# A decoder layer on one core: attention's queries and keys by tokens, one set of angle tables, and retention's gates by turns with the mixer gates

## The chip, the cores and the metric

The kernel runs on one core of one Trainium2 chip. The metric is the device time of one execution in microseconds (us); the figure given is the median of several executions. One further execution of the same program is recorded by the hardware profiler, and all views of the trace come from that one.

## What is computed

One layer for 256 tokens of 2048 features, all in float32: a half feed-forward, a pair of gated token mixers side by side (retention with 8 heads, sliding-window attention with 16 query heads and 4 key heads), a second half feed-forward, and a gated embedding. The part that the change touches, cut from the reference:

```python
rq, rk, rv, rg, aq, ak, av, gate_r, gate_a = jnp.split(h @ w_in[i], SPLIT_POINTS, axis=-1)
# columns: 1024, 1024, 2048, 2048, 1024, 256, 256, 2048, 2048

rq = rotary(rq.reshape(B, S, RET_HEADS, RET_DK), positions, RET_DK, RET_THETA)
rk = rotary(rk.reshape(B, S, RET_HEADS, RET_DK), positions, RET_DK, RET_THETA) * (RET_DK ** -0.5)
ro = head_group_norm(retention_chunkwise(rq, rk, rv), ret_gn_g[i])
ret_branch = (jax.nn.silu(rg) * ro) @ w_ret_out[i]

aq = rotary(aq.reshape(B, S, ATT_HEADS, ATT_DH), positions, ROPE_DIMS, ROPE_THETA)  # 16 of 64
ak = rotary(ak.reshape(B, S, ATT_KV_HEADS, ATT_DH), positions, ROPE_DIMS, ROPE_THETA)
att_branch = sliding_window_attention_sinks(aq, ak, av, att_sinks[i]) @ w_att_out[i]

mixed = (jax.nn.sigmoid(gate_r) * ret_branch + jax.nn.sigmoid(gate_a) * att_branch) @ w_mix_out[i]
```

`rotary` turns pairs of features by an angle that depends on the token's position: all 128 features of a retention head (64 angles), and the first 16 of an attention head (8 angles).

## The kernel before

**Weights.** The weights stream in from memory as tiles of 128 x 1024 floats. For float32 accuracy each is cut in two: ACT casts a high part (L162, tiles named hw), DVE subtracts it from the raw tile for the low part (L164, lw), and PE adds three matmuls for each product (L510 to L512). Where two neighbouring pairs of columns and rows allow it, a unit called Seven makes sums of raw tiles on DVE (L279 to L298; tiles uw, vw, bw and their halves huw, luw, hvw, lvw) and needs seven products in place of eight.

**The planner.** Units of work are planned ahead in a list. `fill` issues a unit's load on SP's queue and, later, its casts, as long as there is room: `slots_for_weights(n)` sets how many tiles may be held (24 for the first stage of the mixers, 14 from rq to the aqk stage, 18 in gt, 22 behind). Casts are issued when less than 45 units of time stand ready, an ordinary tile being 12. After each unit `run_side` takes one step from the list `side` and advances the generators `slow` and `lazy` by one step each. So what a list holds, and in which order the code calls the projections, sets the order on every engine.

**Order of the mixers.** rv01 (two of four blocks of retention's values), rq, rk, rv23, four blocks of retention's gates rg with retention's own steps in `side`, av, five groups aqk (attention's keys, then the queries) with attention's steps in `side`, four blocks gt (columns of the mixer gates), then the gates ga0 and ga1 as blocks with Seven units.

**By tokens and by features.** Most projections are computed by tokens: the tile of tokens is the stationary operand and 512 weight columns stream past. rq and rk are such blocks (`mixer_block`) of 4 x 256 columns with two Seven units each; their result is rotated by tokens (L1393 to L1401) and then turned by a DMA transpose between two passes of ACT (`Turn`, L227, L231, L238), since the scores need features on partitions. aq and ak are computed by features instead (`features_out`, L455 to L490): the weights are stationary and the tokens stream, so that the result has features on partitions at once. A chunk is 8 matmuls over 512 columns, which hold the high and low parts of the 256 tokens (L461), and 8 over 256 columns (L469). `joined` (L1287) adds the two halves, and `turn_by_angle` (L1293 to L1297) rotates with a shuffle of partitions.

**Angle tables.** `rotary_table` (L986) is run once for retention and once for attention: it computes angles for 256 tokens by features, [128 x 256]. Retention's are then transposed on PE (L1378) to have them by tokens.

**Steps.** Retention's head passes through ret1 (scores, L1479), ret1b (decay and split into rsp, L1483), ret2 (outputs ro, L1504) and normalisation; attention through att1 (scores, L1611), att1b (mask and maxima), att1c (Exp, L1633 and L1638), att2 (its transposes, L227 and L231), att2b (outputs ao, L1680) and att3. Silu of rg is at L1576.

Of the kernel before, what the change touches and what calls it, by code (L numbers as in the profile page):

```python
# [70 lines left out]
def layer(ctx: ExitStack, tc: tile.TileContext, io):  # L71
# [281 lines left out]
    def sums_ahead(items, wait, every):  # L353
# [9 lines left out]
        for j, (key, _) in enumerate(items):  # L363
            a, b = pairs.pop()
            b11, b21, b12, b22 = a.of(a.raw, 0), a.of(a.raw, 1), b.of(b.raw, 0), b.of(b.raw, 1)
            u, v = (slot([P, 2, 512], F32, w + a.name) for w in "uv")
            t1, t3, t2, t4 = (x.rearrange("p (g n) -> p g n", g=2) for x in (u[:, 0], u[:, 1], v[:, 0], v[:, 1]))
            parts = [slot([P, 2, 512], F32R, w + a.name) for w in ("hu", "lu", "hv", "lv")]
            uh, ul, vh, vl = parts
            away = [dram.tile([P, 2, 512], F32, name=f"{w}{a.name}") for w in ("hud", "lud", "hvd", "lvd")]  # L370
            put_by_sums[key] = away
            dve.tensor_tensor(t1, b11, b12, ALU.add)
            dve.tensor_tensor(t3, b12, b22, ALU.add)
            yield from pause()
            act.copy(uh, u)
            dve.tensor_tensor(t2, b11, t3, ALU.add)
            dve.tensor_tensor(t4, t2, b21, ALU.add)
            yield from pause()
            act.copy(vh, v)
            if j + 1 < len(items):  # L380
                pairs.append([Chunk(k) for k in items[j + 1]])
            dve.tensor_tensor(ul, u, uh, ALU.subtract)
            yield from pause()
            dve.tensor_tensor(vl, v, vh, ALU.subtract)
            for e in range(2):
                sync.dma_start(away[e], parts[e].bitcast(F32))
            yield from pause()
            for e in range(2, 4):
                sync.dma_start(away[e], parts[e].bitcast(F32))
# [62 lines left out]

    def features_chunk(key, n_k, rhs, ps):
        c, chunks = key[-1], n_k // 4
        u = take(key)  # L455
        hi, lo = u.chunk.hi, u.chunk.lo

        def high(kk):
            k = 4 * c + kk
            for f in range(2):  # L460
                pe.matmul(  # L461
                    ps[f], hi[:, kk, f * P : (f + 1) * P], rhs(k),
                    start=k == 0, stop=k == n_k - 1,
                )

        def low(kk):
            k = 4 * c + kk
            for f in range(2):
                pe.matmul(  # L469
                    ps[f][:, :S], lo[:, kk, f * P : (f + 1) * P], rhs(k)[:, :S],  # L470
                    start=False, stop=False,
                )

        for kk in range(3):
            high(kk)
        if c < chunks - 1:
            high(3)
            for kk in range(4):
                low(kk)
        else:  # L480
            for kk in range(4):
                low(kk)
            high(3)
        done(u)
        run_side()

    def features_out(groups, n_k, rhs, before=None):

        for c in range(n_k // 4):
            if before is not None:
                before(c)
            for key, ps in groups:
                features_chunk(key + (c,), n_k, rhs, ps)
# [146 lines left out]

    def plan_features(keys, n_k):
        for c in range(n_k // 4):
            for key in keys:
                plan.append(Single(key + (c,)))
# [322 lines left out]
    trig = {}  # L969
# [16 lines left out]
    def rotary_table(nm):  # L986

        inv, sgn = (0, 2) if nm == "r" else (1, 3)
        pos_i = slot([P, S], I32, "pos_i" + nm)
        act.dma_start(pos_i, io["positions"].broadcast_to([P, S]))  # L990
        pos = slot([P, S], F32, "pos" + nm)
        yield
        dve.tensor_copy(pos, pos_i)
        table = slot([P, 2, S], F32, "trig" + nm)
        cos, sin = trig[nm] = table[:, 0, :], table[:, 1, :]
        w = slot([P, 4, S], F32, "rot" + nm)
        ang, n, na, nb = (w[:, j, :] for j in range(4))
        dve.tensor_scalar(ang, pos, cst[:, inv : inv + 1], None, ALU.mult)
# [6 lines left out]
        for who, j in ((na, 0), (nb, 0), (na, 1), (nb, 1), (na, 2), (nb, 2), (na, 3)):  # L1005
            dve.scalar_tensor_tensor(ang, who, -TWO_PI[j], ang, ALU.mult, ALU.add)
            if who is nb:
                yield
        yield
        dve.tensor_scalar(n, ang, 3.1415925, -3.1415925, ALU.min, ALU.max)  # L1010
        yield
        act.activation(nb, n, AF.Sin)
        yield
        dve.tensor_scalar(sin, nb, cst[:, sgn : sgn + 1], None, ALU.mult)
        dve.tensor_scalar(na, ang, 1.5707963267948966, None, ALU.add)
        dve.tensor_scalar(n, na, 3.141592653589793, -6.283185307179586, ALU.is_gt, ALU.mult)
        dve.tensor_tensor(na, na, n, ALU.add)
        dve.tensor_scalar(na, na, 3.1415925, -3.1415925, ALU.min, ALU.max)
        yield
        act.activation(cos, na, AF.Sin)  # L1020
# [262 lines left out]
    def joined(ps, name, dst=None):  # L1283
        lo = half(name + "lo")
        v = half(name + "v") if dst is None else dst
        for f in range(2):
            act.copy(lo[:, f], ps[f][:, S:])  # L1287
            dve.tensor_tensor(v[:, f], ps[f][:, :S], lo[:, f], ALU.add)
        return v

    def turn_by_angle(q, name, dst, cos, sin, shuffle):
        qs = half(name + "sh")
        dve.stream_shuffle(qs, q, shuffle)  # L1293
        c, s = (v[:, None, :].broadcast_to([P, 2, S]) for v in (cos, sin))
        dve.tensor_tensor(q, q, c, ALU.mult)
        dve.tensor_tensor(qs, qs, s, ALU.mult)
        dve.tensor_tensor(dst, q, qs, ALU.add)  # L1297

    def rotate(ps, name, dst, cos, sin, shuffle):
        turn_by_angle(joined(ps, name), name, dst, cos, sin, shuffle)  # L1300

    SH_R = [(i + 16) % 32 for i in range(32)]
    SH_A = [i + 8 if i < 8 else i - 8 if i < 16 else i for i in range(32)]
# [3 lines left out]
    QK_UNITS = [units_of(order, SEVEN[: order.count("S")]) for order in ("PPPSPSPP", "PPSPSPPP")]  # L1307
    qk_keys = lambda b: lambda n, p: ("w_in_f2", 4 * b + 2 * n, p)
# [5 lines left out]
    def plan_mixers():  # L1314
        block_units([("P", p) for p in range(KD // 2)], lambda n, p: ("w_rv", n, p))
        for b in range(2):
            block_units(QK_UNITS[b], qk_keys(b))
        for blk in range(2, 4):
            plan_tokens(("w_rv", blk), KD)
        for grp in range(8, 16, 2):  # L1320
            plan_tokens(("w_in_f2", grp), KD)
        plan_tokens(("w_av",), KD, nk=4)
        for grp in (20, 16, 17, 18, 19):
            plan_features([("w_in_f", grp)], KD)
        for grp in range(21, 29, 2):
            plan_tokens(("w_in_f2", grp), KD)
# [16 lines left out]
    def mixers(ht, norm, residual, keepers, away):  # L1343
        rhs = lambda k: (ht[:, k, :S], ht[:, k, S:])
        both_halves = lambda k: ht[:, k, :]
        rq, rk = [], []
        made = {}
        forms = lambda p: made[p // 2](p % 2)
        sums_of, wide = {}, {}
# [23 lines left out]
        def wide_tables():  # L1373
            cos, sin = trig["r"]
            ps = bank("rtab").rearrange("p (w t n) -> p w t n", w=2, t=2)
            for j, v in enumerate((cos, sin)):
                for t in range(2):
                    pe.transpose(ps[:, j, t], v[:, t * P : t * P + P], ident)  # L1378
            for j, w in enumerate("cs"):
                wide[w] = slot([P, 2, 512], F32, f"rtab{w}")  # L1380
                for t in range(2):
                    act.copy(
                        wide[w][:, t].rearrange("p (h n) -> p h n", h=4), ps[:, j, t][:, None, :].broadcast_to([P, 4, P])
                    )

        def rotated(v, name, to):
            halves = lambda x: x.rearrange("p t (q two n) -> p two (t q) n", two=2, n=16)
            crossed = {}

            def cross():  # L1390
                x = crossed["x"] = slot([P, 2, 512], F32, name + "x")
                for two in range(2):
                    dve.tensor_tensor(  # L1393
                        halves(x)[:, two], halves(v)[:, 1 - two], halves(wide["s"])[:, two], ALU.mult
                    )

            def scale():
                dve.tensor_tensor(v, v, wide["c"], ALU.mult)

            def add():  # L1400
                dve.tensor_tensor(v, v, crossed.pop("x"), ALU.add)  # L1401
                crossed["t"] = Turn(v, name)

            def join():
                to.append(slot([P, 4, S], F32, name + "t"))
                crossed.pop("t").join(to[-1])

            return [
                cross, scale, add, lambda: crossed["t"].part(), lambda: crossed["t"].move(), idle, join,
            ]  # L1410
# [708 lines left out]
```

## Time and profile before

| | |
|---|---|
| median of 3 runs | 2221.23 us (2220.66 to 2221.66) |
| profiled execution | 2221.96 us, of which the span of the trace is 2220.0 us |
| mixers' first stage (rv01) to the end of gt | 692.5 to 1138.2 us |
| rq, rk | 737.80 to 780.46, 780.46 to 822.62 us |
| rv23 | 822.62 to 866.14 us |
| rg with retention | 866.14 to 968.28 us |
| av, aqk with attention, gt with attention | to 979.80, 1039.56, 1138.17 us |

A row of a view begins with the engine or the place in time; L12 is a line of the kernel; names such as hw_in_f are the program's tiles, with an arrow from what an instruction reads to what it writes. PE's rows of matmuls overlap, so that the distance between starts (0.23 us for 512 columns) and not the length shown (0.39) is what one costs. SPq is the queue that SP issues DMAs from.

### The profile page before, as it was taken

To read this page: it belongs to the slowest core of one execution; us is meant where nothing else is said; L and a number is where in the kernel's file an instruction comes from. 1 tells how busy PE (TensorE), PEld (TensorE's weight loads), DVE (VectorE), ACT (ScalarE), POOL (GpSimd) and SP (SyncE) were. 2 spreads that over 40 slices of the span, in tenths; PEclk is the share of its full clock that TensorE was granted. 3 is DMA by queue.
4 is the path that set the end of the run, shared out by engine and by line. 5 is a ranking of instruction groups with operands and counts; after the bars stand their busy time and mean duration, and the time that the engine had idled before them with its cause. 6 is when DMAs were issued, how large, how long until landed. Compare 5 with 4: busy or idle time off the path is not lost.

```text
span 2220.0 us, 28845 instructions
## 1 busy us (share of the span) xinstructions
PE 2209.2 (100%) x9980; PEld 1825.5 (82%) x9980; DVE 2021.5 (91%) x2620; ACT 1475.5 (66%) x1706; POOL 48.4 (2%) x62
## 2 busy tenths in 40 slices
PE   9999999999999999999999999999999999999998
PEld 7888888888888888888788888888888878888887
DVE  6999999999988997998999888779999999899887
ACT  5877777777565656666866566466767678765653
POOL 0000000000000000000000000000000000000000
PEclk9999999999999999999999999999999999999999
DMA  9989889977686779886977478788899988767771
GB/s 316 271 224 266 248 246 258 252 241 237 222 301 231 260 266 324 271 296 219 302 223 242 166 226 328 298 299 276 289 314 312 289 264 268 215 236 240 282 291 70
DMA packets 315754, 576.00 MB, mean 259 GB/s; under 512 B 107084, under 2 KB 112076, under 8 KB 315608
## 3 DMA queue, kind: packets, MB, share of 16 engines
q1 hardware_dynamic: 305992, 543.79, 73.0%
q0 software_dynamic: 7632, 27.79, 6.7%
q10 hardware_dynamic: 1984, 2.58, 0.3%
q8 instruction: 78, 1.28, 0.2%
q14 instruction: 68, 0.56, 0.1%
HBM read 490.20 MB, written 33.55 MB: 236 GB/s over the span
## 4 chain that ended last, share of the span: by engine, by line
PE 94%; DMA 3%; DVE 2%; ACT 1%; issue 1%; SPq 0%; ACTq 0%; DVEq 0%
PE f1g L510 3%; PE f1g L512 3%; PE f1g L511 3%; PE f2g L510 2%; PE f1u L511 2%; PE f1u L510 2%; PE f1u L512 2%; PE f2g L511 2%; PE f2g L512 2%; PE f2u L512 2%; PE f2u L510 2%; PE f2u L511 2%; PE aqk L461 2%; PE f1e L512 1%; PE f2d L510 1%; PE f1d L512 1%
## 5 line engine op out<-in xcount | busy, mean ns | idle before, releaser
L164 DVE TENSOR_TENSOR lf_gu<-rf_gu,hf_gu 128x1024 fp32r<-128x1024 f32 x123 | 145.3, 1219 | 17.9 <-ACT hf_gu L162 17.2
L164 DVE TENSOR_TENSOR lw_in_f<-rw_in_f,hw_in_f 128x1024 fp32r<-128x1024 f32 x124 | 148.5, 1218 | 11.2 <-ACT hw_in_f L162 11.2
L162 ACT CAST hf_gu<-rf_gu 128x1024 fp32r<-128x1024 f32 x123 | 123.6, 1048 | 24.8 <-DMA rf_gu<-in_f_gu 24.8
L284 ACT CAST huf_gu<-uf_gu 128x1024 fp32r<-128x1024 f32 x83 | 87.3, 1052 | 76.7 <-DVE uf_gu L280 65.5
L293 ACT CAST hvf_gu<-vf_gu 128x1024 fp32r<-128x1024 f32 x83 | 87.5, 1054 | 76.0 <-DVE vf_gu L289 65.7
L164 DVE TENSOR_TENSOR lf_down<-rf_down,hf_down 128x1024 fp32r<-128x1024 f32 x96 | 115.8, 1220 | 22.3 <-ACT hf_down L162 18.8
L162 ACT CAST hw_in_f<-rw_in_f 128x1024 fp32r<-128x1024 f32 x124 | 125.8, 1048 | 11.3 <-DMA rw_in_f<-in_w_in_f 7.7
L162 ACT CAST hf_down<-rf_down 128x1024 fp32r<-128x1024 f32 x96 | 98.4, 1049 | 29.5 <-DMA rf_down<-in_f_down 13.4
L298 DVE TENSOR_TENSOR lvf_gu<-vf_gu,hvf_gu 128x1024 fp32r<-128x1024 f32 x83 | 101.0, 1217 | 0.0
L296 DVE TENSOR_TENSOR luf_gu<-uf_gu,huf_gu 128x1024 fp32r<-128x1024 f32 x83 | 101.0, 1217 | 0.0
L287 DVE TENSOR_TENSOR lf_gu<-rf_gu,hf_gu 128x1024 fp32r<-128x1024 f32 x83 | 101.0, 1217 | 0.0
L277 ACT CAST hf_gu<-rf_gu 128x1024 fp32r<-128x1024 f32 x83 | 86.8, 1046 | 5.9 <-DMA rf_gu<-in_f_gu 3.2
L510 PE MATMUL f1g<-hf_gu,xt 128*128 128x512 f32 x223 | 87.0, 390 | 1.4 <-ACT hf_gu L113 1.4
L512 PE MATMUL f1g<-lf_gu,xt 128*128 128x512 f32 x223 | 86.9, 390 | 0.0
L511 PE MATMUL f1g<-hf_gu,xt 128*128 128x512 f32 x223 | 86.8, 389 | 0.0
L510 PE MATMUL f2g<-hf_gu,ht 128*128 128x512 f32 x196 | 76.4, 390 | 0.0
L512 PE MATMUL f2g<-lf_gu,ht 128*128 128x512 f32 x196 | 76.3, 389 | 0.0
L511 PE MATMUL f2g<-hf_gu,ht 128*128 128x512 f32 x196 | 76.3, 389 | 0.0
L510 PE MATMUL f1u<-hf_gu,xt 128*128 128x512 f32 x180 | 70.0, 389 | 0.0
L511 PE MATMUL f1u<-hf_gu,xt 128*128 128x512 f32 x180 | 70.0, 389 | 0.0
L512 PE MATMUL f1u<-lf_gu,xt 128*128 128x512 f32 x180 | 70.0, 389 | 0.0
L182 POOL DMA_DIRECT2D lf_gu<-rf_gu x37 | 32.2, 871 | 1630.4 <-ACT lf_gu L181 1365.3
(1640 smaller groups left out, 7310.0 us busy)
## 6 DMA issues: line engine op xcount, KB each, us to landing
rf_gu<-in_f_gu SPq DMA_DIRECT2D x362, 512.0 KB
rf_down<-in_f_down SPq DMA_DIRECT2D x176, 512.0 KB
rw_in_f<-in_w_in_f SPq DMA_DIRECT2D x148, 512.0 KB
lf_gu<-rf_gu POOLq DMA_DIRECT2D x37, 512.0 KB, 8.6
rw_rv<-in_w_rv SPq DMA_DIRECT2D x32, 512.0 KB
rw_ret<-in_w_ret SPq DMA_DIRECT2D x32, 512.0 KB
rw_mix<-in_w_mix SPq DMA_DIRECT2D x32, 512.0 KB
rw_pg<-in_w_pg SPq DMA_DIRECT2D x32, 512.0 KB
```

Of the source, the lines that this page charges most:

```text
L162: act.copy(c.hi, c.raw)
L164: dve.tensor_tensor(c.lo, c.raw, c.hi, ALU.subtract)
L277: act.copy(a.hi, a.raw)
L284: act.copy(uh, u)
L287: dve.tensor_tensor(a.lo, a.raw, a.hi, ALU.subtract)
L293: act.copy(vh, v)
L296: dve.tensor_tensor(ul, u, uh, ALU.subtract)
L298: dve.tensor_tensor(vl, v, vh, ALU.subtract)
L461: pe.matmul(ps[f], hi[:, kk, f * P : (f + 1) * P], rhs(k), start=k == 0, stop=k == n_k - 1,)
L510: pe.matmul(o, al, bh, start=first, stop=False)
L511: pe.matmul(o, ah, bh, start=False, stop=False)
L512: pe.matmul(o, ah, bl, start=False, stop=self.left == 0)
```

## The change

1. aq (1024 columns) becomes a third block by tokens behind rk, with two Seven units; ak (256 columns) follows it, also by tokens, as 96 matmuls of 256 columns. Both are rotated by tokens and then turned by DMA transposes (three more of these). The functions for projections by features are gone.
2. One generator, `rotary_tables`, computes all 72 angles by tokens, [128 x 144], at the start; it spreads the inverse frequencies over tokens by two PE transposes. The second pass for attention, which ran beside rg, is gone.
3. The order is rv01, rq, rk, aq, ak, rv23, av, and then rg0, gt0, rg1, gt1, rg2, gt2, rg3, gt3. All steps of retention and attention lie in one list of 72 places, of which one is taken after each unit from av on. Room for weights is 16 tiles in ak and rv23, and 12 from av to gt3.
4. The side work `sums_ahead` (sums of the second feed-forward's weights, stored to memory and read later) makes three in rq, rk and aq, three in ak, rv23 and av, and four within rg and gt; its tiles are taken one at a time. All of gt's results are copied by ACT, where DVE did two of four. The decay tables load one at a time.

```diff
+    QK_UNITS = [units_of(order, SEVEN[: order.count("S")]) for order in ("PPPSPSPP", "PPSPSPPP", "PPSPSPPP")]
+    qk_keys = lambda b: lambda n, p: ("w_in_f2", (0, 4, 16)[b] + 2 * n, p)
...
+        for b in range(3):
+            name = ("rq", "rk", "aq")[b]
+            got = mixer_block(name, QK_UNITS[b], qk_keys(b), rhs)
...
+            side.extend(both_rotated(got, name, (rq, rk, aq)[b], name[0]))
+        slots_for_weights(16)
+        akv = slot([P, 4, S], F32, "akv")
+        ps = banks("ak")
+        tokens_out(("w_in_f", 20), KD, rhs, ps, n=256)
...
+        side.extend(rotated(ak, "ak", lambda: akv[:, 0:2, :], "a"))
...
-        for grp in (20, 16):
-            attention_features(grp)
...
+        more = sums_ahead(ahead[6:10], 0, 1)
+        at = [[] for _ in range(72)]
+        for m in range(8):
+            for j, part in zip((0, 2, 4, 5, 6, 8, 11), (att1, att1b, att1c, att2, att2a, att2b, att3)):
+                at[1 + 8 * m + j].append(part(m))
+        for c in range(4):
+            h = 2 * c
+            for j, part in (
+                (0, ret1(h)), (2, ret1b(h)), (2, ret1(h + 1)), (4, ret1b(h + 1)), (4, ret2(h)), (7, ret2(h + 1)),
+                (8, ret2b(c)), (12, ret2c(c)), (14, ret3(c)), (15, ret3a(c)), (19, ret3b(c)),
+            ):
+                at[4 + 16 * c + j].append(part)
...
+        slots_for_weights(12)
+        slow.append(spread_out())
...
+        for j in range(4):
+            ps = banks(f"rg{j}")
+            paired_out(("w_in_f2", 8 + 2 * j), KD, rhs, ps)
...
+                act.activation(g[:, t], ps[t], AF.Silu)
...
+            ps = banks(f"gt{j}")
+            paired_out(("w_in_f2", 21 + 2 * j), KD, rhs, ps)
+            sig.append(slot([P, 2, 512], F32, f"sig{j}"))
...
+                act.copy(sig[-1][:, t], ps[t])
```

PE, at the attention queries. Before, the first chunk by features behind av (numbers at the ends of names count buffers):

```order
L512 MATMUL av_8715<-lw_av_8667,ht_5993 128x256
L461 MATMUL aqk_8849<-ht_5993,hw_in_f_0_8740 128x512
L461 MATMUL aqk_8850<-ht_5993,hw_in_f_0_8740 128x512
L461 MATMUL aqk_8849<-ht_5993,hw_in_f_0_8740 128x512
...
L469 MATMUL aqk_8849<-ht_5993,lw_in_f_0_8741 128x256
L469 MATMUL aqk_8850<-ht_5993,lw_in_f_0_8741 128x256
L469 MATMUL aqk_8849<-ht_5993,lw_in_f_0_8741 128x256
```

Now, the first of the queries' rows, directly behind rk's last (aqa and aqb are the two halves of tokens):

```order
L472 MATMUL rka_6907<-lw_in_f_6_7_7191,ht_5993 128x512
L470 MATMUL rkb_6909<-hw_in_f_6_7_7190,ht_5993 128x512
L471 MATMUL rkb_6909<-hw_in_f_6_7_7190,ht_5993 128x512
L472 MATMUL rkb_6909<-lw_in_f_6_7_7191,ht_5993 128x512
L470 MATMUL aqa_7296<-hw_in_f_16_2_7211,ht_5993 128x512
L471 MATMUL aqa_7296<-hw_in_f_16_2_7211,ht_5993 128x512
L472 MATMUL aqa_7296<-lw_in_f_16_2_7212,ht_5993 128x512
L470 MATMUL aqb_7298<-hw_in_f_16_2_7211,ht_5993 128x512
L471 MATMUL aqb_7298<-hw_in_f_16_2_7211,ht_5993 128x512
L472 MATMUL aqb_7298<-lw_in_f_16_2_7212,ht_5993 128x512
```

The queries have moved from behind av to behind rk, weights and tokens have changed places, and each is now three wide matmuls.

ACT, beside the attention's Exp of one head group. Before, within aqk (the load of the table with Exp stands here and nowhere else in this part of the program; aes and asc are the sink's and the scores' tiles):

```order
L162 CAST hw_in_f_0_9202<-rw_in_f_0_9088 128x1024
L1633 ACT_TABLE_LOAD
L1633 ACTIVATE aes_9149<-aes_9149 128x4
L1638 ACTIVATE asc_9140,asm_9209<-asc_9140,anm_9147 128x128 x2
L1638 ACTIVATE asc_9140,asm_9209<-asc_9140,anm_9147 128x256 x2
L162 CAST hw_in_f_1_9230<-rw_in_f_1_9110 128x1024
L162 CAST hw_in_f_2_9258<-rw_in_f_2_9132 128x1024
L227 COPY wat_9264<-asc_9140 128x768 x2
```

Now, between rg1 and gt1 (23_3 is the gates' weight tile, rgs the Silu of retention's gate):

```order
L162 CAST hw_in_f_23_3_9090<-rw_in_f_23_3_9029 128x1024
L1556 ACTIVATE aes_9049<-aes_9049 128x4
L1561 ACTIVATE asc_9040,asm_9097<-asc_9040,anm_9047 128x128 x2
L1561 ACTIVATE asc_9040,asm_9097<-asc_9040,anm_9047 128x256 x2
L1654 ACT_TABLE_LOAD
L1654 ACTIVATE rgs_9117<-rg_8853 128x512
L1654 ACTIVATE rgs_9117<-rg_8854 128x512
L162 CAST hw_in_f_23_4_9134<-rw_in_f_23_4_9067 128x1024
```

Exp and Silu now stand next to each other, and a table load goes ahead of each change from one to the other.

SP, where gt ends and the first Seven unit of the gates (tiles 29_0 and 31_0) is loaded. Before:

```order
L127 DMA rw_in_f_29_4_10261<-in_w_in_f 128x2x512
L386 DMA hudf_gu_0_4_10085<-huf_gu_0_4_10081 128x1024
L386 DMA ludf_gu_0_4_10086<-luf_gu_0_4_10082 128x1024
L127 DMA rw_in_f_31_4_10288<-in_w_in_f 128x2x512
L127 DMA rw_in_f_29_5_10319<-in_w_in_f 128x2x512
L389 DMA hvdf_gu_0_4_10087<-hvf_gu_0_4_10083 128x1024
L389 DMA lvdf_gu_0_4_10088<-lvf_gu_0_4_10084 128x1024
L127 DMA rw_in_f_31_5_10342<-in_w_in_f 128x2x512
L231 DMA_TRANSPOSE mat_10344<-wat_10321 128x12x128
L127 DMA rw_in_f_29_0_10362<-in_w_in_f 128x2x512
L127 DMA rw_in_f_31_0_10364<-in_w_in_f 128x2x512
```

Now (mro is retention's transposed output; hudf to lvdf are sums stored for later):

```order
L127 DMA rw_in_f_29_4_10238<-in_w_in_f 128x2x512
L127 DMA rw_in_f_31_4_10271<-in_w_in_f 128x2x512
L231 DMA_TRANSPOSE mat_10273<-wat_10240 128x12x128
L127 DMA rw_in_f_29_5_10299<-in_w_in_f 128x2x512
L127 DMA rw_in_f_31_5_10318<-in_w_in_f 128x2x512
L231 DMA_TRANSPOSE mro_10358<-wro_10339 128x16x128
L388 DMA hudf_gu_0_4_10095<-huf_gu_0_4_10243 128x1024
L388 DMA ludf_gu_0_4_10096<-luf_gu_0_4_10276 128x1024
L393 DMA hvdf_gu_0_4_10097<-hvf_gu_0_4_10275 128x1024
L393 DMA lvdf_gu_0_4_10098<-lvf_gu_0_4_10360 128x1024
L127 DMA rw_in_f_29_0_10385<-in_w_in_f 128x2x512
L127 DMA rw_in_f_31_0_10387<-in_w_in_f 128x2x512
```

The loads of 29_0 and 31_0 now stand behind both transposes and the four stores, which are not spread among the earlier loads any more.

More of the change, by code (lines that the diff above doesn't have):

```diff
@@ L451, in run_side @@
                 jobs.pop(0)
[L453 to L495, printed above, removed]
     class Sum:
@@ L1700, in mixers @@
[L1700 to L1704 removed]
+            for j, part in zip((0, 2, 4, 5, 6, 8, 11), (att1, att1b, att1c, att2, att2a, att2b, att3)):
[7 more added lines that the diff above has]
+                at[4 + 16 * c + j].append(part)
+            for j in (6, 10, 11, 15):
+                at[4 + 16 * c + j].append(lambda: next(more, None))
+            if c < 3:
+                at[4 + 16 * c + 9].append(lambda c=c: load_decay(c + 1))
@@ new lines, in mixers, with spread_out @@
+        at[67].append(lambda: next(more, None))
+        for step in range(2):
+            at[4 + 3 * 16 + 10 + step].append(lambda step=step: forms_step(1, step))
+        def spread_out():
+            for jobs in at:
+                for f in jobs:
+                    f()
+                yield
+        slots_for_weights(12)
+        slow.append(spread_out())
+        ps = banks("av")
+        tokens_out(("w_av",), KD, rhs, ps, n=256)
+        for t in range(2):
+            dve.tensor_copy(akv[:, 2 + t, :], ps[t][:, :S])
```

285 lines of the change are left out of this document (117 added, 168 removed).

## The prediction

> **What bounds the kernel now.** I read the page's head first, then its chain of work that ended last, then TensorE's waits, and then a table of busy time by stage.
>
> ```profile
> span 2220.0 us, 28845 instructions
> PE 2209.2 (100%) x9980; PEld 1825.5 (82%) x9980; DVE 2021.5 (91%) x2620; ACT 1475.5 (66%) x1706; POOL 48.4 (2%) x62
> PE 94%; DMA 3%; DVE 2%; ACT 1%; issue 1%; SPq 0%; ACTq 0%; DVEq 0%
> ```
>
> PE is busy for 2209.2 of 2220.0 us and holds 94% of the chain. So the time is PE's own work plus about 11 us, and an edit counts only by PE work that it removes, or by a wait on PE that it makes. All weights reach PE through ACT (the rounded high part) and DVE (the rest), and DVE stands at 91%: it is the engine that can become late. In the stages that the change rearranges, PE waits for one thing alone (the rows of waits: what waited for what, us in total, times, longest):
>
> ```profile
> PE ro L1504 <- DVE rsp L114: 0.5, 1, 0.5
> DVE lw_in_f L164 <- ACT hw_in_f L162: 9.7, 13, 2.3
> ```
>
> The first row is the only PE wait from 690 to 1180 us; the second is DVE's own wait from 866.1 to 1138.2 us, needed below. The stages, as a table (stretch, length, then busy us and instructions of PE, weight loads, DVE, ACT, POOL, granted clock, DMA share, GB/s):
>
> ```profile
> 780.50:822.60 42.10, 42.10 (x187) 34.88 (x186) 41.83 (x48) 28.14 (x29) 0.00 (x0) 1.00 0.73 230
> 866.10:968.30 102.20, 101.67 (x490) 85.37 (x490) 95.57 (x186) 65.03 (x81) 0.00 (x0) 1.00 0.86 289
> 968.30:979.80 11.50, 11.50 (x98) 11.50 (x97) 10.83 (x24) 7.18 (x11) 0.00 (x0) 1.00 0.59 236
> 979.80:1039.60 59.80, 59.80 (x355) 51.25 (x353) 50.14 (x84) 38.23 (x63) 0.00 (x0) 1.00 0.73 243
> 1039.60:1138.20 98.60, 98.60 (x483) 77.71 (x481) 90.86 (x163) 79.46 (x139) 0.00 (x0) 1.00 0.95 292
> ```
>
> They are: retention's keys (rk); rg with retention; av; the old queries and keys by features (aqk); the mixer gates (gt) with attention. PE is full in each. The clock was granted in full (1.00). In rk DVE is full as well, 41.83 of 42.10.
>
> **PE work: queries and keys by tokens.** The old form, from the chain (start, us, what):
>
> ```profile
> 979.96 1.84 PE aqk L461 x8
> 981.80 0.95 PE aqk L469 x8
> 982.75 1.84 PE aqk L461 x8
> ```
>
> A chunk is 8 wide and 8 narrow matmuls, 1.84 + 0.95 = 2.79 us. There are 5 groups of 4 chunks: 20 x 2.79 = 55.8 us. The new queries are a third block with two units of seven products in place of eight, as rk is: 186 matmuls, so the length of rk's row, 42.1. The new keys are 96 narrow matmuls, as av is: 11.5. That is 53.6, so **-2.2 us**. It is the only large term that is sure; it rests on counts and on rows of the same shapes.
>
> **Small PE terms.** The angle tables lose two of four transposes:
>
> ```profile
> 746.13 0.44 PE rtab L1378 x4
> ```
>
> so -0.2. Attention's and retention's small matmuls break into the stream of weights. Where that happens:
>
> ```profile
> 1137.04 0.39 PE L512 MATMUL gt<-lw_in_f,ht 128*128 128x512 f32 x1
> 1137.36 0.66 PE L1680 MATMUL ao<-apt,akv 128*64 128x256 f32 x4
> 1138.17 0.50 PE L510 MATMUL ga0a<-hw_in_f,ht 128*128 128x512 f32 x1
> ```
>
> From 1137.04 to 1137.36 is 0.32 us against 0.23 from one wide matmul to the next, so a changeover costs some 0.1. The scores of one head group and the outputs of another no longer stand together, which makes three more interruptions: **+0.3**. Retention's own waits may go:
>
> ```profile
> 934.55 0.56 DVE rsp L114
> 935.15 1.34 PE ro L1504 x9
> 939.24 1.07 PE ro L1504 x9
> ```
>
> One group took 1.34 for 1.07 behind DVE's rsp, and with the 0.5 of the wait row that is about 0.8 in the stage. With two more steps between scores and outputs I take **-0.8**; if DVE is as late as before it is 0, and the same wait at all eight groups would be +4. PE work and its old waits sum to -2.2 - 0.2 + 0.3 - 0.8 = **-2.9**.
>
> **What DVE must now do in a row: rq, rk, aq.** So far the values' projection, light on DVE, followed rk. Now a third block of the same kind does. How far DVE is ahead shows in the end of a low part and PE's first use of it, in three pairs:
>
> ```profile
> 772.54 1.22 DVE L164 TENSOR_TENSOR lw_in_f<-rw_in_f,hw_in_f 128x1024 fp32r<-128x1024 f32 x1
> 780.91 0.39 PE L512 MATMUL rka<-lw_in_f,ht 128*128 128x512 f32 x1
> 800.61 1.22 DVE L298 TENSOR_TENSOR lvw_in_f<-vw_in_f,hvw_in_f 128x1024 fp32r<-128x1024 f32 x1
> 803.35 0.39 PE L512 MATMUL rks<-lvw_in_f,gaf0h 128*128 128x512 f32 x1
> 817.01 1.22 DVE L164 TENSOR_TENSOR lw_rv<-rw_rv,hw_rv 128x1024 fp32r<-128x1024 f32 x1
> 823.07 0.39 PE L512 MATMUL rv<-lw_rv,ht 128*128 128x512 f32 x1
> ```
>
> The lead is 780.91 - 773.76 = 7.15 us at rk's start, 803.35 - 801.83 = 1.52 behind its second unit of seven, and 823.07 - 818.23 = 4.84 at its end. rk thus spends 5.6 of lead in its middle. If aq starts with 4.84 and spends the same (rk's rotation falls in it, as rq's falls in rk), PE stands for 5.6 - 4.84 = 0.8. The lower bound is 0, since the sums made on the side are spread otherwise. The upper is 4: aq begins with nothing ahead but what the first plain units win back (about 2). I take **+0.7**, near the pairs.
>
> **av, then rg and gt by turns, with every step of both mixers beside them.** The room for weights falls from 14 and 18 to 12. Loads run 6 units ahead, not 8, a unit of 12 matmuls being 12 x 0.227 = 2.7 us; the casts keep their distance of 4 units. What DVE drops with the old form:
>
> ```profile
> L164 DVE TENSOR_TENSOR lw_in_f<-rw_in_f,hw_in_f 128x1024 fp32r<-128x1024 f32 x22 | 26.1, 1219 | 3.0 <-ACT hw_in_f L162 3.0
> L1288 DVE TENSOR_TENSOR ra0v<-aqk,ra0lo 128x256 f32<-128x256 f32 x2 | 0.8, 420 | 1.8 <-ACT ra0lo L1287 1.8
> L1293 DVE STREAM_SHUFFLE ra0sh<-ra0v 128x512 f32<-128x512 f32 x1 | 0.8, 751 | 0.0
> L1296 DVE TENSOR_TENSOR ra0sh<-ra0sh,triga 128x512 f32<-128x512 f32 x1 | 0.7, 683 | 0.0
> ```
>
> Over the four old stages DVE was busy 95.57 + 10.83 + 50.14 + 90.86 = 247.4 us. Off go 26.1 of low parts and five rotations of 0.8 + 0.8 + 3 x 0.7 = 3.7, 18.5 in all. 203 remain for a stretch of 102.2 + 11.5 + 98.6 = 212.3: 96%. That hides in PE's time with 9 us left. If the cover goes, each us over is one of PE's. ACT: 189.9 before, less 20 casts and the copies (about 24), plus what follows.
>
> ```profile
> 1014.90 1.06 ACT L162 CAST hw_in_f<-rw_in_f 128x1024 fp32r<-128x1024 f32 x1
> 1015.98 1.28 ACT L1633 ACT_TABLE_LOAD   x1
> 1017.27 0.21 ACT L1633 ACTIVATE aes<-aes 128x4 f32<-128x4 f32 x1
> ```
>
> Silu and Exp now alternate on ACT, 8 table loads instead of 1: 7 x 1.28 = 9.0 us. ACT then stands at about 176 of 212 us (83%), so I cost them at nothing; the cover is the lead of the casts, 4 units or 11 us, against two loads that stand at most a few us apart. The cast before the load ended at 1015.96 and the next instruction began at 1017.27, so the row holds the whole price here.
>
> The Trainium skill, page "ScalarE: Activation LUTs", section "Table sets: the hidden batching unit", speaks against this change: "Batch activation calls by **set**, not by function". Its section "What ACT_TABLE_LOAD costs" puts a drain of some 1.38 us on top of the load; the trace shows the load's 1.28 us and no drain. By the page the seven switches would be an estimated 18.6 us of ACT, which would still fit.
>
> For the whole stretch I take **+0.2**: 0 below, 5 above.
>
> **Gates' first unit of seven.** In the new order its two raw tiles wait for a place that the last gt unit frees, and stand behind two transposes and four stores on SP's queue. Before:
>
> ```profile
> 1128.21 1.71 SPq L231 DMA_TRANSPOSE mat<-wat  x1
> 1130.01 17.57 SPq L127 DMA_DIRECT2D rw_in_f<-in_w_in_f  x8
> 1139.05 1.05 ACT L277 CAST hw_in_f<-rw_in_f 128x1024 fp32r<-128x1024 f32 x1
> 1142.69 1.22 DVE L287 TENSOR_TENSOR lw_in_f<-rw_in_f,hw_in_f 128x1024 fp32r<-128x1024 f32 x1
> 1149.68 0.39 PE L512 MATMUL ga0s<-lw_in_f,ht 128*128 128x512 f32 x1
> ```
>
> Issue was at 1130.01, the cast at 1139.05, the low part ready at 1143.91, used at 1149.68: 19.7 us from issue to use, 5.8 of them spare. Now the issue comes about when gt ends (1138.17, above), 11.5 before the use: 8.2 later against 5.8 spare, 2.4 late if the chain keeps its length. But the cast stood behind one that waited for PE, not for its data, so the chain can be shorter. Bounds 0 and 4; I take **+1.0**. The three more DMA transposes (1.71 on SP each) stand in stretches where loads are 6 units ahead: 0.
>
> **Sum.** -2.9 + 0.7 + 0.2 + 1.0 = -1.0 us. From the profiled execution's 2221.96 (span 2220.0 and 2.0 around it) that is 2221.0; the median of the runs, 2221.23, lies 0.7 below that execution, so the forecast is **2220.2**.
>
> **Rivals.**
> 1. *All stalls hidden.* The three waits of 0.7, 0.2 and 1.0 don't come: -2.9, so 2218.3. For it: one PE wait in 490 us so far. Against: leads of 1.5 us. Chance 0.22.
> 2. *The gates' unit or aq's block late in full*, +4 at one of them: -1.0 + 3 is 2223.2. Chance 0.14.
> 3. *Slower: DVE the bound in rg and gt.* It needs 203 of 212.3 us; its waits for ACT's casts were 9.7 in these stages. With table loads and all steps ahead of casts those waits could double, to 203 + 19 = 222, 10 over, of which the lead at the start (some 4) is spent first: +6, so 2226.2. It decides where DVE's waits pass 13 us, the 9 free and the lead of 4. For it: DVE at 95.57 of 102.20 already. Against: steps are spread evenly, which shortens waits. Chance 0.14.
> 4. *Slower: ACT switching.* The casts come late by the loads themselves; all seven on PE's path would be +9.0, 2229. Against: ACT keeps 36 us free. Chance 0.04. That is the case that the Trainium skill's rule on sets would make.
> 5. *The saving isn't there*, because the third block or the new keys take as long as the old form: +2.2, 2222.4. Counts and equal shapes speak against. Chance 0.04.
>
> **How the numbers follow.** The forecast has 0.42, the rivals 0.22, 0.14, 0.14, 0.04 and 0.04. About 0.2% (4.4 us) is what a measurement of this kernel can tell from no change. Faster by more needs under 2216.8, beyond even the first rival: 0.06. Slower by more needs over 2225.7: most of rival 3, rival 4 and a little of rival 2, 0.18. The rest, 0.76, is within. The range runs from 2217.0 (rival 1 with another 1.3 of interruptions saved) to 2226.8 (rival 3 with its place).
>
> **What would show it.** Right: aq's block takes 42 to 43 us and ak 11.5; the row of PE waiting for rsp is gone; the table loads stand beside a PE without waits; PE's waits in ga0 are under 2 us. Wrong: waits of PE for lw_in_f in aq (third term), for lw_in_f or hw_in_f within rg and gt (rivals 3 and 4, told apart by whether DVE waits for ACT there), or a wait at the first ga0s matmul above 3 (rival 2). What would make the whole wrong is a stall spread in pieces too small for rows of waits: then PE's stages are longer than their counts at 0.227 a matmul.

## The result

The changed kernel takes 2252.0 us (median of 4 runs, 2250.3 to 2253.5) against 2221.3 us before: 1.0138 times as long, interval 1.0121 to 1.0156. It is 31 us slower, where 1 us faster was forecast, and lies outside the range. The profiled execution took 2251.16 us. The head of its page and its chain:

```profile
span 2249.1 us, 28774 instructions
PE 2218.7 (99%) x9940; PEld 1826.0 (81%) x9940; DVE 2008.3 (89%) x2593; ACT 1496.3 (67%) x1730; POOL 48.3 (2%) x62
PE 77%; DVE 4%; DMA 4%; ACT 2%; issue 1%; SPq 0%; ACTq 0%; DVEq 0%
```

PE has fallen from 94% of the chain to 77%, though DVE has less to do than before and ACT, with 20.8 us more, is busy for only 67% of the span: the sum of the work is not what made it slower. PE is shown busy for 9.5 us more with fewer matmuls, so some of them ran longer. The largest of its waits from 865 to 1210 us, where before had one of 0.5:

```profile
PE as L1534 <- ACT akv L238: 4.9, 1, 4.9
PE ga0s L470 <- ACT hw_in_f L277: 4.4, 1, 4.4
PE ga0s L472 <- DVE lw_in_f L287: 3.9, 3, 2.2
PE ro L1469 <- DVE rsp L114: 3.2, 3, 2.0
PE ga0s L472 <- DVE luw_in_f L296: 1.4, 1, 1.4
PE rv L472 <- DVE lw_rv L164: 1.1, 1, 1.1
```

And rows of the table by stage: ga0 before, then, in the changed kernel, aq, av, the third rg block and ga0:

```profile
1138.20:1179.10 40.90, 40.90 (x182) 33.85 (x181) 40.26 (x50) 25.21 (x29) 0.00 (x0) 1.00 0.64 211
821.20:865.10 43.90, 42.70 (x187) 34.73 (x186) 42.64 (x51) 28.63 (x30) 0.00 (x0) 1.00 0.91 282
921.50:941.30 19.80, 14.86 (x106) 13.93 (x106) 15.93 (x24) 16.15 (x26) 0.00 (x0) 0.83 1.03 340
1043.50:1073.10 29.60, 27.61 (x139) 22.12 (x138) 21.17 (x42) 23.98 (x38) 0.00 (x0) 1.00 0.94 297
1148.50:1209.30 60.80, 49.98 (x189) 36.74 (x189) 48.21 (x58) 35.26 (x43) 0.00 (x0) 0.89 0.66 225
```

av has 11.5 us of weight matmuls and lasts 19.8; ga0 took 41.0 before and takes 60.8. In both the granted clock is below 1, 0.83 and 0.89. From the first matmul of rv01 to the last of ga0, by the starts of PE's rows:

| part | before | after | difference |
|---|---|---|---|
| rv01, rq, rk | 130.1 | 129.9 | -0.2 |
| aqk's own matmuls, now aq and ak | 56.4 | 55.5 | -0.9 |
| rv23 | 43.5 | 44.9 | +1.4 |
| av's own matmuls | 11.5 | 18.1 | +6.6 |
| rg, gt and all small matmuls up to gt's end | 204.2 | 208.9 | +4.7 |
| ga0 | 41.0 | 60.8 | +19.8 |
| sum | 486.7 | 518.1 | +31.4 |

The rest of the program, which the change does not touch, is 2.2 us shorter in this execution, so the two profiled executions differ by 29.2. Two stages hold 26 of the 31 us.

**ga0.** What SP did around gt's end, at 1148.5 us (start, us, queue, line, DMA):

```profile
1141.37 1.44 SPq L231 DMA_TRANSPOSE mat<-wat  x1
1142.91 1.39 SPq L127 DMA_DIRECT2D rw_in_f<-in_w_in_f  x2
1152.68 1.76 SPq L231 DMA_TRANSPOSE mro<-wro  x1
...
1157.19 1.11 SPq L393 DMA_DIRECT2D lvdf_gu<-lvf_gu  x1
1158.39 6.59 SPq L127 DMA_DIRECT2D rw_in_f<-in_w_in_f  x8
```

The queue issues in order. Nothing leaves it from 1144.3 to 1152.68, because the transpose of retention's last output waits for ACT's copy of it, which ends at 1152.65. From there the queue issues without a pause: the transpose and the four stores take it until 1158.3 (the low part that the last store reads is ready at 1156.0, before the queue comes to it). Only then, 9.9 us after gt's end, come the eight loads for the gates: 4.1 us of this are the wait, the rest is the issue of the five DMAs. ACT can cast the first tile 6 us later:

```profile
1164.63 1.04 ACT L277 CAST hw_in_f<-rw_in_f 128x1024 fp32r<-128x1024 f32 x1 [9.93 <-DMA rw_in_f<-in_w_in_f]
```

ACT had stood for 9.93 us with nothing to cast, DVE for 10.05, and PE waits seven times in the rest of the stage. Of the 19.8 us, 10.8 are waits of PE and 0.8 are attention's last outputs, which now fall in ga0; the other 8.2 us are its products themselves, which run longer, in part at half the granted clock (last section).

**av.** The chain of waits at the end of rv23 and in av:

```profile
908.13 11.03 DMA rf_gu<-in_f_gu
...
921.85 0.15 DVE ak L1363
922.26 0.35 issue
922.62 0.61 ACT wak L227
923.26 7.77 DMA mak<-wak
931.08 0.61 issue
931.68 0.75 ACT akv L238
932.48 0.80 PE as L1534 x4
```

rf_gu is a raw tile of the second feed-forward, for a sum that is only stored for later. DVE, in order, stood for 5.7 us at that sum with the keys' rotation behind it. The keys were then turned late, and the first scores of attention, which stand in PE's order ahead of the rest of av, held PE for 4.9 us. The window from 865 to 945 us has three such waits on DVE:

```profile
DVE uf_gu L372 <- DMA rf_gu<-in_f_gu: 14.8, 3, 7.7
```

So two queues that work in order, SP's and DVE's, each held something urgent behind something that was not. That is the theory to test; its rival is that DVE or ACT has too much to do in the new order. Against the rival stands already that from av to gt's end, 227.0 us, DVE is busy for 179.7 and ACT for 165.5.

### The profile page after: what moved, and what is told of

It reads as the page before. It is cut to its first block, busy times and chain, and to the rows that moved or that the text cites. A ratio compares the mean times of both kernels' runs of the same rounds, so it can differ in the third digit from the quotient of the medians.

```text
span 2249.1 us, 28774 instructions
## 1 busy us (share of the span) xinstructions
PE 2218.7 (99%) x9940; PEld 1826.0 (81%) x9940; DVE 2008.3 (89%) x2593; ACT 1496.3 (67%) x1730; POOL 48.3 (2%) x62
## 3 DMA queue, kind: packets, MB, share of 16 engines
q8 instruction: 78, 1.28, 0.2%
## 4 chain that ended last, share of the span: by engine, by line
PE 77%; DVE 4%; DMA 4%; ACT 2%; issue 1%; SPq 0%; ACTq 0%; DVEq 0%
PE f2g L472 2%; PE f2g L471 2%; PE f2g L470 2%; PE f2u L472 2%; PE f2u L470 2%; PE f2u L471 2%; DMA rw_in_f<-in_w_in_f 1%; PE f2e L472 1%; PE f2e L470 1%; PE f1e L472 1%; PE f2d L470 1%; PE f1e L470 1%; PE f1d L470 1%; PE f2d L471 1%; PE f1d L471 1%; PE f1d L472 1%
## 5 line engine op out<-in xcount | busy, mean ns | idle before, releaser
L279 DVE TENSOR_TENSOR uf_gu<-rf_gu 128x512 f32<-128x512 f32 x83 | 56.8, 684 | 12.6 <-DMA rf_gu<-in_f_gu 9.3
```

## Experiments

All are made from the changed kernel unless said; before was timed beside each (medians 2221.5 us for experiments 1 to 4, 2222.2 for 5 to 8, 2221.7 for 9 to 11). Stages are read from one profiled execution of each kernel.

**1. Room for the gates' loads.**

```diff
             ps = banks(f"gt{j}")
+            if j == 3:
+                slots_for_weights(16)
```

> The changed kernel with room for 16 weight tiles in place of 12 from the last gt block on. Theory A (the loads of the gates' first unit of seven stand too late in SP's queue, behind a transpose and four stores, because there is no room for them sooner): they now stand ahead of those, PE's waits in ga0 fall from about 10.8 us to under 2, ga0 takes 41 to 44 us in place of 60.8, and the time falls by 16 to 19 us, to 2233 to 2236. Rival (ACT or DVE cannot keep up with rg and gt by turns, and ga0 only pays what they left undone): casts and low parts are late whatever is loaded, ga0 stays above 50 us, the time above 2242.

Measured: 2243.2 us, ratio to before 1.0097 (1.0082 to 1.0112). The first loads of the unit of seven were issued at 1145.3, ahead of the transpose of retention's output, and the wait of 4.4 us is gone. But only half of the expected gain came:

```profile
1152.50:1201.60 49.10, 46.12 (x189) 35.70 (x188) 46.56 (x57) 33.54 (x41) 0.00 (x0) 0.93 0.74 249
```

DVE is at 46.56 of 49.10 here: with the queue mended, the retention and attention steps that had slipped into ga0 fill it. The rival has a share in this stage: the time is where it had put it, ga0 just under its 50 us.

**2. The queue's order alone.** Room stays 12; retention's last transpose and the last stored sums go five places later.

```diff
-                at[4 + 16 * c + j].append(part)
+                at[4 + 16 * c + j + (5 if c == 3 and j > 13 else 0)].append(part)
...
-                at[4 + 16 * c + j].append(lambda: next(more, None))
+                at[4 + 16 * c + j + (5 if c == 3 and j > 10 else 0)].append(lambda: next(more, None))
...
-        at[67].append(lambda: next(more, None))
+        at[73].append(lambda: next(more, None))
```

> The changed kernel, room still 12, with retention's last transposes five places later and the last stored sums five places later, so that both stand behind the loads of the gates' first unit of seven in SP's queue. Theory A in its narrow form (the queue's order, not the room): the loads issue when gt ends instead of 10 us later, ga0 takes 43 to 50 us, the time is 2235 to 2242. Rival (room for 12 tiles alone makes the unit late): ga0 stays within 3 us of 60.8, the time at 2249 or more.

Measured: 2242.3 us, 1.0094 (1.0079 to 1.0109), at the edge of what was expected; ga0 lasts 46.9 us. The loads left at 1150.6, 2.8 us ahead of gt's end in that execution, with room for 12 as before. So the small room was not by itself what made them late: it is enough to move those DMAs, with the steps on ACT and DVE that feed them, behind the loads, and more room is another way round them. The time fell by less than ga0 did (9.7 against 13.9 us). In the profiled execution part of the difference is in av, which took 22.7 us with a wait of 8.3 for akv, though the edit touches nothing ahead of it: that wait differs between executions.

**3. Attention's first scores three places later.**

```diff
-                at[1 + 8 * m + j].append(part(m))
+                at[1 + 8 * m + j + (max(0, 3 - j) if m == 0 else 0)].append(part(m))
```

> The changed kernel with attention's first scores and their mask three places later, all else where it was. Theory B (the scores stand in PE's order before the keys have been turned, and PE waits): the wait of 4.9 us for akv goes and so does the half clock behind it, av takes 11.5 to 14 us in place of 19.7, the time falls by 5 to 8 us to 2244 to 2247. Rival (DVE and ACT are late there anyhow, and PE meets the next wait): under 2 us are won.

Measured: 2248.2 us, 1.0118 (1.0103 to 1.0133), 4 us won, less than the theory's 5 to 8. PE's wait for akv is gone and av takes 12.6 us, but the first rg block grew from 26.4 to 30.4. Some 1.2 of this is the moved scores' own work (the block takes 27.6 us in experiment 5, without waits); the rest is a wait of 2.7 us for rsp. The keys are still late: ACT stands for 3.1 us at their copy with three casts of weights behind it, and DVE waits 3.4 us for these. So PE, as far as these rows show, meets the same lateness at the next place.

**4. The raw tiles of stored sums loaded sooner.**

```diff
             dve.tensor_tensor(t4, t2, b21, ALU.add)
+            if j + 1 < len(items):
+                pairs.append([Chunk(k) for k in items[j + 1]])
             yield from pause()
...
-            if j + 1 < len(items):
-                pairs.append([Chunk(k) for k in items[j + 1]])
             yield from pause()
```

> The changed kernel with the raw tiles of each next stored sum loaded two pauses sooner. Theory B2 (the keys are late because DVE stands in order behind a sum whose raw tiles have not landed: 14.8 us of DVE waits for rf_gu from 865 to 945 us): the first item of each list stays as it was, the others' waits go, DVE's waits for rf_gu fall under 8 us, PE's wait for akv under 1.5 us, and the time falls by 4 to 8 us to 2244 to 2248. Rival (the place of the scores alone decides): the wait for akv stays above 3.5 us and the time within 2 us of 2252.

Measured: 2241.3 us, 1.0088 (1.0071 to 1.0105), 11 us won, more than expected. DVE's waits for these tiles fell to the one that the edit leaves:

```profile
DVE uf_gu L372 <- DMA rf_gu<-in_f_gu: 7.8, 1, 7.8
PE as L1534 <- ACT akv L238: 1.4, 1, 1.4
```

and PE's waits for rsp, 3.2 us in rg, went too: the second, third and fourth rg blocks take 27.4 us each instead of 27.9, 29.7 and 28.6. There the loads for stored sums had held another queue, SP's. DVE's three waits for rf_gu all lie ahead of 945 us, none in rg or gt. But ahead of the longest wait for rsp in the changed kernel, SP issued two of these loads before four weight tiles, and ACT stood for a weight tile with its half of rsp's split behind it:

```profile
1049.04 2.13 SPq L127 DMA_DIRECT2D rf_gu<-in_f_gu  x2
1051.26 2.26 SPq L127 DMA_DIRECT2D rw_in_f<-in_w_in_f  x4
1058.03 1.05 ACT L162 CAST hw_in_f<-rw_in_f 128x1024 fp32r<-128x1024 f32 x1 [4.55 <-DMA rw_in_f<-in_w_in_f]
1060.45 0.51 ACT L113 CAST rsp<-rsc 128x384 fp32r<-128x384 f32 x1
1061.60 0.51 PE L1469 MATMUL ro<-rvh,rsp 128*128 128x256 f32 x2 [1.99 <-DVE rsp L114]
```

In experiment 4 the two loads are not at this place, and ACT stands there for 2.04 us. ga0 is nearly as long as in the changed kernel (58.3 us).

**5. All four mended.** Experiments 1, 3 and 4 together, and retention's last turn back moved behind the gates.

```diff
-                (8, ret2b(c)), (12, ret2c(c)), (14, ret3(c)), (15, ret3a(c)), (19, ret3b(c)),
+                (8, ret2b(c)), (12, ret2c(c)), (14, ret3(c)), (15, ret3a(c)), (19 if c < 3 else 42, ret3b(c)),
```

> The changed kernel with the edits of the runs before together (room for 16 from the last gt block, attention's first scores three places later, the sums' raw tiles loaded two pauses sooner) and retention's last turn back (ret3b of the last pair of heads) moved from ga0 into the stage behind the gates. Theory: the stalls are apart and their gains add: 9 + 11 + 2, and 3 to 5 more as ga0 no longer carries the last 4.3 us of ACT and 1.7 of DVE: 2224 to 2230, ga0 at 42 to 46 us. Rival (each mended stall uncovers the next): above 2234.

Measured: 2226.9 us (10 runs), 1.0019 (1.0010 to 1.0029): as expected, 26 of the 31 us are back. ga0 takes 44.8 us, av 11.5. No wait of PE is over 2 us, there is none from av to gt's end, and the mean clock of the execution is 1.000 against 0.995. It is still slower than before, by 4.7 us.

**6. More table loads.** On top of experiment 4.

```diff
                 act.activation(g[:, t], ps[t], AF.Silu)
+            act.activation(warm, warm, AF.Exp)
+            act.activation(warm, warm, AF.Silu)
```

> The changed kernel with the sums' raw tiles loaded sooner (2241.3 us as measured), and behind each Silu pair an Exp and a Silu of one column more on ACT, which makes 8 table loads more in rg and gt: some 8 x (1.28 + 0.4) = 13 us of ACT. Theory (ACT has time in rg and gt, the switches cost nothing there): the time stays within 2 us of 2241.3. Rival (the switches are what made rg and gt longer): 8 to 14 us slower, 2249 to 2255.

Measured: 2251.2 us, 1.0130 (1.0115 to 1.0145), some 9 us slower than experiment 4. The theory fell: sixteen loads are not hidden. The eight added ones cost two thirds of their 13 us of ACT, with new waits in rg and gt:

```profile
PE ro L1469 <- DVE rsp L114: 3.5, 2, 2.0
PE gt L472 <- DVE lw_in_f L164: 2.9, 3, 1.9
```

**7. The four rg ahead of the four gt.** On top of experiment 4; the list of steps is unchanged.

```diff
             gate_v.append(g)
+        for j in range(4):
             ps = banks(f"gt{j}")
```

> The changed kernel with the sums' raw tiles loaded sooner (2241.3 us), and the four rg blocks one after another ahead of the four gt blocks; the steps of retention and attention stay where they are in their list. Fewer changes of table on ACT. Theory (by turns or not decides nothing, what decides is what stands in the queues at av and at the gates): within 3 us of 2241.3, PE waits in ga0 as before. Rival (alternating costs): 5 us faster or more.

Measured: 2241.7 us, 1.0087 (1.0072 to 1.0102), no difference to experiment 4, and ga0 at 58.9 us. So the order of the blocks by turns costs nothing that shows. But the edit did not take switches away, though that had been expected: Exp still falls between the Silus of the rg blocks, and this kernel has nine table loads from 860 to 1150 us where experiment 4 has eight. That the eight cost nothing is seen elsewhere. Experiments 4 and 5 have all eight, and no wait of PE from rg0 to gt's end. For av, rg and gt together experiment 5 takes 216.1 us and experiment 8, which has one load there, 215.9. With experiment 6, the cover was there for eight and not for sixteen.

**8. The first two parts of the change alone.** Queries and keys by tokens and one set of angle tables, with experiment 4's loads; behind them the order and room of before and nearly its steps (retention's as they were, attention's four places apart; the stored sums in lists of three, five and two).

```diff
+        slots_for_weights(14)
+        two_heads(0)
+        for h in range(0, HR, 2):
...
+        begin = [2, 6, 10, 14, 18, 22, 26, 30]
...
+        ps = banks("av")
...
+        slots_for_weights(18)
```

> The first two parts of the change alone: queries and keys by tokens behind rk, angle tables once, and the sums' raw tiles loaded sooner; but the order of before behind them (rg with retention's steps, av, gt with attention's steps, four places for each head group) with its room of 14 and 18 tiles. Theory (the saving on PE of some 2 us is real, and the loss comes from the new order, its room and its queues): 2217 to 2222, ga0 at 41 to 42 us. Rival (the third block of products in a row, or attention in a shorter stretch, makes DVE late): 2224 or more, with waits in aq or gt.

Measured: 2223.4 us (10 runs), 1.0005 (0.9996 to 1.0015): no difference to before, just above the theory's 2222 and under the rival's 2224, and 28 us better than the whole change; 11 of these came with experiment 4's loads already, the rest with the order, steps and room. aq took 42.9 us, ak 11.5. The loss is in the other parts. ga0 took 43.3 us instead of 41 to 42, with attention's tail and a wait of 1.0 us in it.

**9. Attention's steps ending within gt**, three and a half places apart, on top of experiment 8.

```diff
-        begin = [2, 6, 10, 14, 18, 22, 26, 30]
+        begin = [1, 4, 8, 11, 15, 18, 22, 25]
```

> As the kernel with the first two parts alone and the order of before (e8_part, 2223.4 us beside 2222.2 of before on its chip), with attention's steps three and a half places apart in place of four and one place earlier, so that they end within gt and the outputs of one head group stand with the scores of another. Theory (what e8_part lost is attention's tail in ga0, 1.5 us of waits, and separate interruptions): 2 to 3 us faster than e8_part, 0.3 to 1.5 us faster than before. Rival (attention in a shorter stretch makes DVE or ACT late in gt): slower than e8_part, with PE waits in gt.

Measured: 2221.9 us (11 runs) beside 2221.7, 0.9998 (0.9989 to 1.0007). ga0 takes 40.8 us again, but it is not faster than before. By the ratios it is some 1.5 us under experiment 8, where 2 to 3 were expected; whether it beats it can't be told, since the intervals overlap.

**10. One stored sum fewer beside rq, rk and aq**, on top of experiment 9.

```diff
-        lazy.append(sums_ahead(ahead[:3], 3, 3))
-        lazy.append(sums_ahead(ahead[3:8], 6, 2))
+        lazy.append(sums_ahead(ahead[:2], 3, 3))
+        lazy.append(sums_ahead(ahead[2:8], 14, 2))
```

> As e9_earlier, with two stored sums in place of three beside rq, rk and aq, and six in place of five beside the values. Theory (the third block in a row costs 0.7 us because DVE is full): aq falls from 42.9 to 42.2 us and the time by 0.5 to 1 us against e9_earlier. Rival (the six sums later cost as much): no difference.

Measured: 2221.2 us (11 runs) beside 2221.7, 0.9997 (0.9988 to 1.0006). aq falls from 43.7 to 42.16 us, exactly rk's length, and the view of PE's waits from 865 to 1210 us is empty. The time is no different from experiment 9's within the intervals. From rv01 to ga0's end PE takes 485.1 us against 486.7 before: the saving is there on PE, and it is too small to show in the time.

**11. Work in place of PE's wait in ga0.** 28 matmuls into a bank that is not read, ahead of the first product of seven.

```diff
+            if j == 2:
+                ps = bank("cover")
+                for k in range(28):
+                    pe.matmul(ps, ht[:, k % 8, :P], ht[:, k % 8, :], start=k == 0, stop=k == 27)
```

> The changed kernel with 28 wide matmuls on PE into a bank that nobody reads, ahead of the first product of seven in ga0, where PE waits for 4.4 and then 2.2 us; they add 6.4 us of PE work and leave nothing out. Theory C (a wait of some us is followed by some 3 us at half the granted clock, which is lost on top of the wait): PE does not stand, the clock stays at 1.00 there, and the time falls by 2 to 4 us although work was added. Rival (the clock is not tied to the wait, or the work only adds): the time is the same or up to 6 us longer.

Measured: 2251.7 us, 1.0137 (1.0121 to 1.0152), the time of the changed kernel. By the time alone it is the rival's case. The profile has the rest:

```profile
1161.35 6.51 PE L1668 MATMUL cover<-ht 128*128 128x512 f32 x28
1148.70:1207.10 58.40, 51.95 (x217) 38.54 (x216) 45.77 (x55) 35.18 (x43) 0.00 (x0) 1.00 0.67 226
```

The clock is 1.00 over the stage, not 0.89, and ga0 is 2.3 us shorter (58.4 against 60.8) with 6.5 us more work in it. PE's waits there fell from 10.8 to 6.4 us, none above 1.4. So the added work cost nothing there: it stood where PE had waited, and the slow clock went away. That the whole time did not fall leaves the gain of 2 us unproven in runs that spread by 5.

## Why the prediction was wrong

**The PE work was counted rightly.** aq at 42.1 and ak at 11.5 us are what experiment 10 shows, 42.16 and 11.51. The old form is 56.4 by starts, not 55.8, so the term is -2.7 rather than -2.2. The terms for transposes and changeovers are too small to be read one by one. Rival 5 is out.

**Step "rq, rk, aq in a row": right, sized low.** The term was +0.7; the changed kernel shows 43.95 us for aq, +1.8, with 1.2 us of waits for low parts, and the runs from 42.2 to 44.2. It is DVE's load from stored sums, as experiment 10 shows by taking one away.

**Step "retention's waits go", -0.8: wrong in sign.** They grew to 3.2 us in three waits, within the upper end given. More steps between scores and outputs did not help, because the lateness did not come from DVE's own work: casts on ACT stood for weight tiles, and in the case shown SP had issued loads for a stored sum ahead of these. The waits vanish with those loads sooner (experiment 4).

**Step "av, then rg and gt by turns", +0.2: this failed.** I set DVE's busy time against the stretch, 203 of 212 us, and took 9 us free as cover. The work was indeed far below that limit (179.7 of 227.0 us); but an engine in order does not spend free time where it likes. The change loads a stored sum's raw tiles one pause later, and lets the second list start one unit after its first load in place of twelve; this stands in the diff, and the prediction gives it no price. What stands behind the waiting sum on DVE I did not list, though the keys' rotation is there, and behind that PE's scores. It cost 6.6 us in av, and the same loads on SP's queue most of the 4.7 in rg and gt. Rival 3 had DVE late, by waits for casts. Its sign came: from 865 to 1150 us these waits are 25.3 us, not 9.7 and beyond its 13. But they are not what PE paid for. Experiment 4 leaves them at 25.1 us and wins 11, and PE waits for no low part in rg or gt.

**Step "gates' first unit of seven", +1.0 with 4 at most: this failed most, 19.8 us.** The place was right, and the rows of SP's order were in front of me. I assumed that the loads issue when gt ends. They left 9.9 us later, because I gave the transpose and the four stores ahead of them nothing: neither the wait for ACT's copy of retention's last output, 4.1 us beyond gt's end, nor their own issue, 5.7 us. Experiment 2 shows this by moving them. Rival 2 had the place and the sign, a wait at the first ga0s matmul above 3 us (it was 4.4), and priced it at 4. That upper end was also too low in kind. It took one lateness, where the stage then ran without any lead: the first wait of 4.4 us was followed by six more waits, by steps that share ga0 with the gates (experiments 1 and 5), and by two stretches of half clock.

**Step "table loads cost nothing": right for eight,** wrong as a margin. I had ACT at 83% and 36 us free; eight more loads cost 9 of their 13 us. The eight of the changed kernel took 1.28 us each, and where the next instruction on ACT did not wait for DVE it began 0.01 us behind the load. Rival 4 did not happen, but its chance of 0.04 was too low for so thin a cover.

**What stays open.** The mended version of the new order is 4.7 us above before. In its profiled execution ga0 alone is 3.8 us longer than before, with 1.6 us of waits for DVE's low parts and 0.8 of attention's outputs; which step would have to move was not tried. How much of the 31 us is the slow clock is bounded only by the profile: from aq to ga0 three stretches of 6.8 us at half, so 10.2 us there at most, and less by what PE waited in them anyhow.

## What to carry to other kernels

For each DMA or vector instruction that a change puts ahead of an urgent one on the same queue, price when it can start as well as how long its issue takes: list what it waits for and the latest time at which that is ready. Side work that fills free time on an engine working in order must have its data there well before its turn, or it makes that engine's free time someone else's wait. Count the lead in front of a stage as part of its cost: a stage with no lead gives back any lateness several times over.

## What was not expected of the hardware

Around waits of PE the granted clock fell to half. In the changed kernel's profile it did so three times, for 6.8 us each (from 930.3, 1165.8 and 1196.5 us). In ga0 (same columns as the table by stage):

```profile
1163.00:1166.00 3.00, 0.28 (x1) 0.28 (x2) 0.00 (x0) 1.04 (x1) 0.00 (x0) 0.97 1.00 373
1166.00:1169.00 3.00, 0.90 (x2) 0.18 (x1) 2.96 (x5) 1.66 (x2) 0.00 (x0) 0.50 1.05 397
1169.00:1172.00 3.00, 2.87 (x7) 2.32 (x8) 3.00 (x5) 2.19 (x4) 0.00 (x0) 0.50 1.03 380
```

The seven matmuls in the last stretch start 0.43 us apart instead of 0.23. In av the clock fell 2.8 us into the wait of 4.9 us and came back 4.6 us after its end. The third time it fell behind shorter waits (1.1 and 1.4 us) that followed each other. A single wait of 2.0 us in rg left the clock at 1.00, but in experiment 1 one of 2.1 us in the last rg block was followed by half clock from 1117.1 to 1120.5 us. With the wait in ga0 filled by work (experiment 11) it stayed at 1.00 there. So a stall of PE can cost more than its length here, and its length alone does not tell whether it will.

The Trainium skill, page "TensorE: Matmul & The Clock Gate", section "Part 1: The HAM clock gate", gives a half clock after an idle window of some 3.4 us and until about as long a busy one. That the clock fell at the waits of 4.4 and 4.9 us and not at the one of 2.0 agrees with it. That it fell already 2.8 us into the wait in av, and that it fell behind waits of 1.1 and 1.4 us and, in experiment 1, of 2.1 us, is not told by it.
